# Up projection: in every second tile of weights the short matmul is issued before the long one

## The chip, the core and the metric

The kernel runs on one core of one Trainium2 chip. The metric is the device time of one execution in microseconds (us), as the median of the executions shown. The engines are TensorE (PE in the profile; its weight loads have a row of their own, PEld), VectorE (DVE), ScalarE (ACT), GpSimd (POOL) and SyncE (SP), whose queue issues the transfers of the weights.

## What is computed

One transformer block on 256 tokens of width 2048: a mixing part (three attention branches with gates) and a feed-forward part. The change lies in the feed-forward part, in the product `h2 @ w_up`:

```python
h2 = rms_norm(x, g_ffn[l])                                          # 256 x 2048
u = causal_depthwise_conv(h2 @ w_up[l], conv_w[l], conv_b[l])       # w_up: 2048 x 11264
u_gate, u_val = jnp.split(u, 2, axis=-1)
x = x + (jax.nn.silu(u_gate) * u_val) @ w_down[l]
```

All inputs are float32. The kernel splits each float32 operand of a product into a rounded part (hi) and the remainder (lo), both of type fp32r, and adds three products: hi times hi, lo times hi, hi times lo.

## The kernel before

**Tiling of the up projection (lines 729 to 745).** The product is made transposed: the weights are the stationary operand, in tiles of 128 x 128, and the tokens are the moving one. `hT` holds, for each of the 16 tiles of the contraction (`KT`), 512 columns: the hi parts of the 256 tokens and, behind them, their lo parts. The loop over `f0` takes four tiles of output columns at a time, and `s` says whether they belong to the gate half or the value half, so there are 11 x 2 = 22 groups. A group has four PSUM banks, `ps[0]` to `ps[3]`, one for each output tile `i`, and collects the 16 contraction tiles in them. There are eight banks in all, so that two groups can be in hand.

**A pair of matmuls.** For each contraction tile `k + j` and each output tile `i` two matmuls are issued (lines 739 and 740):

- the long one: stationary `hi[:, j, c]`, moving all 512 columns of `hT`; it adds hi times hi into columns 0 to 255 of the bank and hi times lo into columns 256 to 511;
- the short one: stationary `lo[:, j, c]`, moving the 256 hi columns; it adds lo times hi into columns 0 to 255 of the same bank.

Each has its own weight load. So the queue of TensorE reads long, short, long, short, through the whole stage: 22 x 16 x 4 = 1408 pairs. The first matmul into a bank (`start`) is a long one, the last (`stop`) a short one.

**Where the weights come from.** `piece` (lines 130 to 141) brings 512 KB of weights at a time, two contraction tiles by four output tiles, which feed 8 pairs. SyncE's queue issues the transfer into `raw`; ScalarE casts it into `hi` (line 136); VectorE subtracts to get `lo` (line 137). `raw`, `hi` and `lo` have four buffers each (`WBUFS`, `SBUFS`), so the cast for one piece waits until TensorE has done with the `hi` of the piece four back, and the subtraction writes the `lo` buffer of the piece four back. The stage has 22 x 8 = 176 pieces.

**What else runs in the stage.** When a group is complete, `conv` (lines 705 to 727) drains its banks: ScalarE copies columns 256 to 511 out (line 710, tile `cr`), VectorE adds columns 0 to 255 (line 712), and both engines then do the convolution, the gate and the split into `aT`. These steps are handed to `later` and issued piece by piece by `tick`. On ScalarE and VectorE they stand in the same queues as the casts and subtractions. The order on each engine is the order of the program.

**Other stages with the same kind of matmul.** `product` and `passes` (lines 143 to 166) serve the projections before: there the tokens are stationary and the weights move. Three matmuls of one width follow one another into one bank (lines 147, 148, 149), then three into the other. The width is 512 columns in nearly all of them (tiles `g`, `s`, `f`, `o`), 256 in the last product of the `s` tiles (`s4`).

Of the kernel before, what the change touches and what calls it, by code (L numbers as in the profile page):

```python
# [41 lines left out]
def hybrid_block(  # L42
# [25 lines left out]
    nc = tc.nc  # L68
# [12 lines left out]
    def bank(name):  # L81
        return pp.tile([P, 512], F32, tag="bank", name=name)
# [14 lines left out]
    def later(gen):  # L97
        waiting.append(gen)

    def tick():  # L100
        while waiting and len(active) < WINDOW:
            active.append([waiting.popleft(), 0])
        for a in list(active):
            if a[1] > 0:
                a[1] -= 1
                continue
            try:
                a[1] = next(a[0]) or 0
            except StopIteration:
                active.remove(a)  # L110
# [19 lines left out]
    def piece(src, a, n, name):  # L130
        raw = wp.tile([P, PIECE], F32, tag="raw", name=f"raw_{name}")
        hi = wp.tile([P, PIECE], F32R, tag="hi", bufs=SBUFS, name=f"hi_{name}")
        lo = wp.tile([P, PIECE], F32R, tag="lo", bufs=SBUFS, name=f"lo_{name}")
        m = a * n
        nc.sync.dma_start(raw[:, :m].rearrange("p (a n) -> p a n", a=a), src)
        pin(nc.scalar.copy(hi[:, :m], raw[:, :m]))  # L136
        pin(nc.vector.tensor_tensor(lo[:, :m], raw[:, :m], hi[:, :m].bitcast(F32), ALU.subtract))  # L137
        return (
            hi[:, :m].rearrange("p (a n) -> p a n", a=a),
            lo[:, :m].rearrange("p (a n) -> p a n", a=a),  # L140
        )
# [9 lines left out]
    def product(x_of, w, nk, n0, n, name):  # L151

        ps = [bank(f"{name}_{t}") for t in range(NT)]
        wv = w.rearrange("(k p) n -> p k n", p=P)
        for k in range(0, nk, 2):
            a = min(2, nk - k)
            wh, wl = piece(wv[:, k : k + a, n0 : n0 + n], a, n, f"{name}_{k}")
            order = [(j, t) for j in range(a) for t in range(NT)]
            if k + a == nk:
                order.sort(key=lambda jt: jt[1])  # L160
            for j, t in order:
                passes(ps[t][:, :n], x_of(k + j), t, wh[:, j], wl[:, j], k + j == 0, k + j == nk - 1)
            tick()
        return ps
# [278 lines left out]
    ps = proj(C_MQ, MEM_W, "mq")  # L443
# [33 lines left out]
    for c in range(3):  # L477
        ps = proj(c * 512, 512, f"f{c}")
# [7 lines left out]
    ps = proj(1536, 512, "f3")  # L486
# [3 lines left out]
    ps = proj(2048, 262, "f4")  # L490
# [68 lines left out]
    for c in range(3):  # L559
        ps = proj(C_SB + c * 512, 512, f"s{c}")  # L560
# [4 lines left out]
    ps = proj(C_SB + 1536, 512, "s3")  # L565
# [3 lines left out]
    ps = proj(C_SB + 2048, 256, "s4")  # L569
# [61 lines left out]
    for n in range(4):  # L631
        n0 = n * 512
        gate = []
        for b in range(3):
            bg = gp.tile([P, 512], F32, tag="bg", name=f"bg_{n}_{b}")
            nc.sync.dma_start(bg, b_gate[0, b, n0 : n0 + 512].partition_broadcast(P))
            ps = proj(C_GATE + b * D + n0, 512, f"g{n}_{b}")
# [11 lines left out]
        for i, (w, k0, nk, b) in enumerate(branches):  # L649
            ps = product(lambda k: oT[:, k0 + k], w[0], nk, n0, 512, f"b{n}_{b}")  # L650
# [10 lines left out]
    hT = xt_pool.tile([P, KT, 2 * S], F32R, tag="xt", name="hT")  # L661
# [19 lines left out]
    for n in range(4):  # L681
        c = slice(n * 512, (n + 1) * 512)
        ps = product(lambda k: mT[k // 2][:, k % 2], w_out[0], KT, n * 512, 512, f"o{n}")
# [21 lines left out]
    def conv(ps, f, s):  # L705
        if not pads:
            padded()
        ct = s * FT + f
        cr = cp.tile([P, S], F32, tag="cr", bufs=2, name=f"cr_{f}_{s}")
        nc.scalar.copy(cr, ps[:, S:])  # L710
        u = pads[f % 2]
        nc.vector.tensor_tensor(cr, cr, ps[:, :S], ALU.add)
        nc.vector.tensor_tensor(u[:, 2:], cr, rbc, ALU.mult)
        y = cp.tile([P, S], F32, tag="y", bufs=6, name=f"y_{f}_{s}")
        tap = lambda j: taps[:, j, ct : ct + 1]
        nc.scalar.activation(y, u[:, 2:], AF.Identity, scale=tap(2), bias=tap(3))
        nc.vector.scalar_tensor_tensor(y, u[:, 1 : S + 1], tap(1), y, ALU.mult, ALU.add)
        nc.vector.scalar_tensor_tensor(y, u[:, 0:S], tap(0), y, ALU.mult, ALU.add)
        if s == 0:
            nc.scalar.activation(y, y, AF.Silu)  # L720
            ys[f] = y
        else:
            g = ys.pop(f)
            nc.vector.tensor_tensor(g, g, y, ALU.mult)
            split_to(aT[:, f, :], g)
        return
        yield

    for f0 in range(0, FT, 4):
        for s in range(2):  # L730
            ps = [bank(f"u{f0 + i}_{s}") for i in range(4)]
            c0 = s * D_FF + f0 * P
            for k in range(0, KT, 2):
                hi, lo = piece(upv[:, k : k + 2, c0 : c0 + 512], 2, 512, f"u{f0}_{s}_{k}")
                for j in range(2):
                    first, last = k + j == 0, k + j == KT - 1
                    for i in range(4):
                        c = slice(i * P, (i + 1) * P)
                        nc.tensor.matmul(ps[i], lhsT=hi[:, j, c], rhs=hT[:, k + j, :], start=first, stop=False)  # L739
                        nc.tensor.matmul(  # L740
                            ps[i][:, :S], lhsT=lo[:, j, c], rhs=hT[:, k + j, :S], start=False, stop=last
                        )
                tick()
            for i in range(4):
                later(conv(ps[i], f0 + i, s))
# [180 lines left out]
```

## Time and profile before

| | us |
|---|---|
| median of three executions | 1498.22 |
| lowest and highest | 1497.55, 1498.96 |
| span of the profiled execution | 1494.4 |
| first and last start of a matmul of the up projection, in that span | 766.0, 1255.2 |
| TensorE busy in the span | 1483.2 |
| VectorE, ScalarE busy | 1014.0, 794.0 |

The profile gives for each engine the time in which at least one of its instructions was running. Matmuls are pipelined, their ends are modelled, and their times overlap, so the distance from start to start says more about them than their durations. The profiled execution's own time is its span; the device time of an execution is a little longer than the span, and the median stands 3.8 us above it.

### The profile page before, as it was taken

What the parts mean: (1) busy time and instruction counts of PE and PEld (TensorE: products, weight loads), DVE (VectorE), ACT (ScalarE), POOL (GpSimd) and SP (SyncE); (2) the same over time, 40 slices, a digit from 0 to 9 for tenths busy, and PEclk for the clock granted to TensorE, in tenths of its full rate; (3) what the DMA queues carried; (4) which work ended last, traced back from release to release, by engine and by line L of the source; (5) the groups of instructions that cost most, each with busy time, mean ns of one, the idle gap of its engine ahead of it and who ended that gap; (6) DMA issues with size and microseconds to landing.
All of it is one profiled execution on the core that took longest, in us unless ns stands there. A gap on an engine that the chain in (4) does not pass through costs nothing.

```text
span 1494.4 us, 19871 instructions
## 1 busy us (share of the span) xinstructions
PE 1483.2 (99%) x7429; PEld 1255.9 (84%) x7429; DVE 1014.0 (68%) x1465; ACT 794.0 (53%) x1108; POOL 16.1 (1%) x46
## 2 busy tenths in 40 slices
PE   8999999999999999999999999999999999999998
PEld 6888888888888888888888888888888888888777
DVE  5767566555655646555557778777778778987885
ACT  6755454358544444444456556556556656553552
POOL 0000000001000000000000000000000000000000
PEclk9999999999999999999999999999999999999999
DMA  8665475365666666655555665655656565556554
GB/s 291 193 211 158 126 220 167 119 211 164 188 194 210 185 210 203 185 190 190 184 182 183 198 191 184 196 190 184 198 187 191 186 196 183 199 188 228 185 202 140
DMA packets 138543, 283.62 MB, mean 190 GB/s; under 512 B 9275, under 2 KB 18127, under 8 KB 138447
## 3 DMA queue, kind: packets, MB, share of 16 engines
q1 hardware_dynamic: 137118, 280.26, 59.0%
q10 hardware_dynamic: 1328, 2.11, 0.4%
q8 instruction: 58, 0.95, 0.2%
q14 instruction: 39, 0.31, 0.1%
HBM read 280.23 MB, written 2.10 MB: 189 GB/s over the span
## 4 chain that ended last, share of the span: by engine, by line
PE 95%; DMA 2%; ACT 1%; DVE 1%; issue 0%; POOL 0%; SPq 0%; DVEq 0%; POOLq 0%; ACTq 0%
PE u L739 21%; PE u L740 11%; PE g L147 5%; PE g L148 5%; PE g L149 5%; PE x L797 4%; PE x L798 4%; PE x L799 4%; PE s L147 2%; PE s L149 2%; PE f L147 2%; PE f L149 2%; PE s L148 2%; PE f L148 2%; PE o L147 2%; PE o L149 2%
## 5 line engine op out<-in xcount | busy, mean ns | idle before, releaser
L739 PE MATMUL u<-hT,hi_u 128*128 128x512 f32 x1408 | 488.5, 392 | 0.0
L740 PE MATMUL u<-hT,lo_u 128*128 128x256 f32 x1408 | 395.1, 281 | 0.0
L739 PEld LDWEIGHTS u<-hT,hi_u 128*128 128x128 f32 x1408 | 263.3, 187 | 57.3
L137 DVE TENSOR_TENSOR lo_u<-raw_u,hi_u 128x1024 fp32r<-128x1024 f32 x176 | 215.4, 1224 | 116.0 <-ACT hi_u L136 115.9
L740 PEld LDWEIGHTS u<-hT,lo_u 128*128 128x128 f32 x1408 | 266.8, 189 | 0.0
L136 ACT CAST hi_u<-raw_u 128x1024 fp32r<-128x1024 f32 x176 | 184.7, 1050 | 138.4 <-PE u L739 106.5
L137 DVE TENSOR_TENSOR lo_g<-raw_g,hi_g 128x1024 fp32r<-128x1024 f32 x96 | 117.7, 1229 | 101.3 <-ACT hi_g L136 98.8
L136 ACT CAST hi_g<-raw_g 128x1024 fp32r<-128x1024 f32 x96 | 100.7, 1051 | 121.8 <-PE g L148 97.4
L147 PE MATMUL g<-hi_g,xT 128*128 128x512 f32 x384 | 151.1, 393 | 0.0
L149 PE MATMUL g<-lo_g,xT 128*128 128x512 f32 x384 | 149.8, 390 | 0.0
L148 PE MATMUL g<-hi_g,xT 128*128 128x512 f32 x384 | 149.7, 390 | 0.0
L792 ACT CAST hi_d<-raw_d 128x1024 fp32r<-128x1024 f32 (+1 forms) x88 | 86.7, 993 | 74.6 <-PE x L798 38.7
L793 DVE TENSOR_TENSOR lo_d<-raw_d,hi_d 128x1024 fp32r<-128x1024 f32 (+1 forms) x88 | 99.8, 1148 | 16.2 <-ACT hi_d L792 16.2
L797 PE MATMUL x<-hi_d,aT 128*128 128x512 f32 x268 | 104.4, 390 | 0.0
L799 PE MATMUL x<-lo_d,aT 128*128 128x512 f32 x268 | 104.4, 390 | 0.0
L798 PE MATMUL x<-hi_d,aT 128*128 128x512 f32 x268 | 104.4, 390 | 0.0
L149 PEld LDWEIGHTS g<-lo_g,xT 128*128 128x128 f32 x384 | 72.1, 188 | 15.2
L148 PEld LDWEIGHTS g<-hi_g,xT 128*128 128x128 f32 x384 | 72.2, 188 | 14.5
L147 PEld LDWEIGHTS g<-hi_g,xT 128*128 128x128 f32 x384 | 72.2, 188 | 14.6
L137 DVE TENSOR_TENSOR lo_s<-raw_s,hi_s 128x1024 fp32r<-128x1024 f32 (+1 forms) x40 | 44.7, 1118 | 37.2 <-ACT hi_s L136 37.2
L137 DVE TENSOR_TENSOR lo_f<-raw_f,hi_f 128x1024 fp32r<-128x1024 f32 (+1 forms) x40 | 44.7, 1120 | 34.5 <-ACT hi_f L136 33.0
L136 ACT CAST hi_f<-raw_f 128x1024 fp32r<-128x1024 f32 (+1 forms) x40 | 38.5, 966 | 52.5 <-PE f L148 47.6
(318 smaller groups left out, 2554.3 us busy)
## 6 DMA issues: line engine op xcount, KB each, us to landing
raw_u<-in_w_up_dram SPq DMA_DIRECT2D x176, 512.0 KB, 4.0
raw_g<-in_w_in_dram SPq DMA_DIRECT2D x96, 512.0 KB, 3.6
raw_d<-in_w_down_dram SPq DMA_DIRECT2D x88, 512.0 KB, 4.7
raw_f<-in_w_in_dram SPq DMA_DIRECT2D x32, 512.0 KB, 3.5
raw_s<-in_w_in_dram SPq DMA_DIRECT2D x32, 512.0 KB, 3.4
raw_o<-in_w_out_dram SPq DMA_DIRECT2D x32, 512.0 KB, 4.7
raw_kv<-in_w_mem_kv_dram SPq DMA_DIRECT2D x15, 512.0 KB, 5.4
raw_b<-in_w_br_fox_dram SPq DMA_DIRECT2D x12, 512.0 KB, 4.0
```

The lines of the kernel that those rows point to most:

```text
L136: pin(nc.scalar.copy(hi[:, :m], raw[:, :m]))
L137: pin(nc.vector.tensor_tensor(lo[:, :m], raw[:, :m], hi[:, :m].bitcast(F32), ALU.subtract))
L147: nc.tensor.matmul(o, lhsT=xh, rhs=wh, start=first, stop=False)
L148: nc.tensor.matmul(o, lhsT=xl, rhs=wh, start=False, stop=False)
L149: nc.tensor.matmul(o, lhsT=xh, rhs=wl, start=False, stop=last)
L739: nc.tensor.matmul(ps[i], lhsT=hi[:, j, c], rhs=hT[:, k + j, :], start=first, stop=False)
L740: nc.tensor.matmul(ps[i][:, :S], lhsT=lo[:, j, c], rhs=hT[:, k + j, :S], start=False, stop=last)
L792: nc.scalar.copy(hi[:, :n], src)
L793: nc.vector.tensor_tensor(lo[:, :n], src, hi[:, :n].bitcast(F32), ALU.subtract)
L797: nc.tensor.matmul(o, lhsT=ah, rhs=w[0], start=first, stop=False)
L798: nc.tensor.matmul(o, lhsT=al, rhs=w[0], start=False, stop=False)
L799: nc.tensor.matmul(o, lhsT=ah, rhs=w[1], start=False, stop=last)
```

## The change

In the up projection the two matmuls of a pair change places where `i` is 1 or 3, except for the first contraction tile of a group, whose long matmul must come first because it starts the bank.

```diff
                     for i in range(4):
                         c = slice(i * P, (i + 1) * P)
-                        nc.tensor.matmul(ps[i], lhsT=hi[:, j, c], rhs=hT[:, k + j, :], start=first, stop=False)
-                        nc.tensor.matmul(
+                        both = lambda last: nc.tensor.matmul(
+                            ps[i], lhsT=hi[:, j, c], rhs=hT[:, k + j, :], start=first, stop=last
+                        )
+                        half = lambda last: nc.tensor.matmul(
                             ps[i][:, :S], lhsT=lo[:, j, c], rhs=hT[:, k + j, :S], start=False, stop=last
                         )
+                        if first or i % 2 == 0:
+                            both(False)
+                            half(last)
+                        else:
+                            half(False)
+                            both(last)
```

TensorE, the second contraction tile of the first piece. `u_0_6213` to `u_0_6216` are the four banks; `hi_u` and `lo_u` are the two parts of the weights; the last figure is the moving operand, 512 columns for the long matmul and 256 for the short one. A minus is the order before, a plus the order with the change (the short matmul stands on line 740 before and on line 742 now):

```order
 L739 MATMUL u_0_6213<-hT,hi_u_0_0_6218 128x512
-L740 MATMUL u_0_6213<-hT,lo_u_0_0_6219 128x256
+L742 MATMUL u_0_6213<-hT,lo_u_0_0_6219 128x256
+L742 MATMUL u_0_6214<-hT,lo_u_0_0_6219 128x256
 L739 MATMUL u_0_6214<-hT,hi_u_0_0_6218 128x512
-L740 MATMUL u_0_6214<-hT,lo_u_0_0_6219 128x256
 L739 MATMUL u_0_6215<-hT,hi_u_0_0_6218 128x512
-L740 MATMUL u_0_6215<-hT,lo_u_0_0_6219 128x256
+L742 MATMUL u_0_6215<-hT,lo_u_0_0_6219 128x256
+L742 MATMUL u_0_6216<-hT,lo_u_0_0_6219 128x256
 L739 MATMUL u_0_6216<-hT,hi_u_0_0_6218 128x512
-L740 MATMUL u_0_6216<-hT,lo_u_0_0_6219 128x256
```

In the second and the fourth bank the short matmul moved ahead of the long one, so the queue reads long, short, short, long, and again. The last matmul of a piece is now a long one, on `hi`, where it was a short one, on `lo`.

VectorE, the subtractions of the first group's pieces, with what each waits for (the transfer, TensorE, ScalarE):

```order
 L137 TENSOR_TENSOR lo_u_0_6_6319<-raw_u_0_6_6317,hi_u_0_6_6318 128x1024 [waits DMAHW2_49,Activation_49]
-L137 TENSOR_TENSOR lo_u_0_8_6341<-raw_u_0_8_6339,hi_u_0_8_6340 128x1024 [waits DMAHW3_49,PE_49,Activation_49]
-L137 TENSOR_TENSOR lo_u_0_10_6363<-raw_u_0_10_6361,hi_u_0_10_6362 128x1024 [waits DMAHW4_49,PE_49,Activation_49]
+L137 TENSOR_TENSOR lo_u_0_8_6341<-raw_u_0_8_6339,hi_u_0_8_6340 128x1024 [waits DMAHW3_49,Activation_49]
+L137 TENSOR_TENSOR lo_u_0_10_6363<-raw_u_0_10_6361,hi_u_0_10_6362 128x1024 [waits DMAHW4_49,Activation_49]
 L174 SCALAR_TENSOR_TENSOR hT<-hT_6261,gmix_c,hT 128x256 [waits Activation_49]
```

The subtraction no longer waits for TensorE itself: the cast ahead of it waits for the last matmul of the piece four back, which covers both buffers.

ScalarE, the drain of the first group's last two banks and the cast behind it:

```order
 L716 ACTIVATE y_0_6474<-u_6459,taps 128x256 [waits DVE_49]
 L710 COPY cr_0_6501<-u_0_6215 128x256
-L710 COPY cr_0_6510<-u_0_6216 128x256 [waits PE_49]
+L710 COPY cr_0_6510<-u_0_6216 128x256
 L136 CAST hi_u_1_8_6564<-raw_u_1_8_6563 128x1024 [waits DMAHW3_49,PE_49,Activation_49]
```

The order of ScalarE's instructions, and of VectorE's, SyncE's and GpSimd's, is the same as before; only such waits differ. On TensorE no wait moved.

## Prediction

> **What bounds the kernel now.** I read the page from the top: the span, the engines, the chain that ended last, and then the groups of the two lines that the change touches.
>
> ```profile
> span 1494.4 us, 19871 instructions
> PE 1483.2 (99%) x7429; PEld 1255.9 (84%) x7429; DVE 1014.0 (68%) x1465; ACT 794.0 (53%) x1108; POOL 16.1 (1%) x46
> ...
> PE 95%; DMA 2%; ACT 1%; DVE 1%; issue 0%; POOL 0%; SPq 0%; DVEq 0%; POOLq 0%; ACTq 0%
> ...
> L739 PE MATMUL u<-hT,hi_u 128*128 128x512 f32 x1408 | 488.5, 392 | 0.0
> L740 PE MATMUL u<-hT,lo_u 128*128 128x256 f32 x1408 | 395.1, 281 | 0.0
> L739 PEld LDWEIGHTS u<-hT,hi_u 128*128 128x128 f32 x1408 | 263.3, 187 | 57.3
> ...
> L740 PEld LDWEIGHTS u<-hT,lo_u 128*128 128x128 f32 x1408 | 266.8, 189 | 0.0
> ```
>
> TensorE is busy for 99% of the span and makes up 95% of the chain of waits. Both groups of matmuls show an idle time of 0.0 ahead of them. So in this stage nothing is waited for: what counts is how soon one matmul may start after another. The durations 392 and 281 ns don't tell that, since they overlap. I take it from the timeline of the stage, by starts:
>
> ```profile
> 849.73 0.39 PE L739 MATMUL u<-hT,hi_u 128*128 128x512 f32 x1
> 849.96 0.28 PE L740 MATMUL u<-hT,lo_u 128*128 128x256 f32 x1
> 850.08 0.39 PE L739 MATMUL u<-hT,hi_u 128*128 128x512 f32 x1
> ...
> 855.97 0.39 PE L739 MATMUL u<-hT,hi_u 128*128 128x512 f32 x1
> ```
>
> From the first long matmul to the last one here there are 18 pairs in 6.24 us, 346.7 ns a pair. From long to short it is 230 ns, which leaves 116.7 ns from short to long. The view of the tile `u` gives the stage's first and last starts:
>
> ```profile
> L739 PE MATMUL u<-hT,hi_u x1408: 389/391/476, 766.0 to 1255.0; 128*128 128x512 f32 x176
> L740 PE MATMUL u<-hT,lo_u x1408: 277/281/285, 766.2 to 1255.2; 128*128 128x256 f32 x176
> ```
>
> 1408 pairs at 346.7 ns make 488.1 us, and the stage lies between the starts 766.0 and 1255.2, 489.2 us, so it is dense throughout. The view by windows says that the clock has nothing left to give (the column before the DMA share):
>
> ```profile
> 770.00:1250.00 480.00, 480.00 (x2774) 423.72 (x2773) 361.66 (x600) 284.98 (x438) 0.00 (x0) 1.00 0.60 190
> ```
>
> **The change part by part.** No matmul, no load and no transfer is added or removed. Of 1408 pairs, those with `i` 1 or 3 outside the first contraction tile of a group are turned round: 22 groups x 15 tiles x 2 = 660. Each time, a stretch of four matmuls that read long, short, long, short reads long, short, short, long, with a long one behind it. Of the four steps from start to start, one long-to-short (230) and one short-to-long (116.7) stay. The other two, again 230 and 116.7, together 346.7, become a step from short to short and a step from long to long. This stage has neither, but other stages have both.
>
> Short to short: the last product of the `s` tiles runs matmuls of 256 columns alone, the same type and the same size of stationary tile. Their count by the view of the tile `s` (32 on each of three lines, 96), then the first, the second and the last by the timeline:
>
> ```profile
> L149 PE MATMUL s<-lo_s,xT x160: 282/390/399, 196.4 to 309.6; 128*128 128x512 f32 x128, 128*128 128x256 f32 x32
> ...
> 298.21 0.28 PE L147 MATMUL s<-hi_s,xT 128*128 128x256 f32 x1
> 298.33 0.28 PE L148 MATMUL s<-hi_s,xT 128*128 128x256 f32 x1
> ...
> 309.61 0.28 PE L149 MATMUL s<-lo_s,xT 128*128 128x256 f32 x1
> ```
>
> 95 steps in 11.40 us are 120.0 ns each. Here three matmuls in a row add into one bank before the other bank's turn, so the step holds within a bank and from bank to bank.
>
> Long to long: a dense piece of the gate projections, 99 matmuls of 512 columns, first and last:
>
> ```profile
> 539.63 0.39 PE L147 MATMUL g<-hi_g,xT 128*128 128x512 f32 x1
> ...
> 561.85 0.39 PE L149 MATMUL g<-lo_g,xT 128*128 128x512 f32 x1
> ```
>
> 98 steps in 22.22 us are 226.7 ns each.
>
> So the two new steps cost 120.0 + 226.7 = 346.7 ns, and the two that they replace cost 346.7 ns. **The sum is 660 x 0.0 = 0.0 us.** This is more than a coincidence of two numbers. 256 further columns cost 226.7 - 120.0 = 106.7 ns, so 256 columns alone take 106.7 and each matmul has 13.3 ns on top, whatever its width. A pair of unlike neighbours, as it runs today, costs exactly a long one among long ones plus a short one among short ones. The 230 where 226.7 would be expected, and the 116.7 where 120.0 would be, are 3.3 ns that the short one starts later and the next long one gets back. In these rows the cost of a matmul does not depend on its neighbour.
>
> The bounds of the two unknown steps, by the nearest rows. Short to short: 120.0 by the same shape elsewhere; 116.7 if it behaves like today's short-to-long. Long to long: 226.7 by the same shape elsewhere; 230 if it behaves like today's long-to-short. The low end is 116.7 + 226.7 = 343.4, a gain of 3.3 ns or 2.2 us over 660 places. The high end is 120.0 + 230 = 350, a loss of 3.3 ns or 2.2 us. I take the middle, since those rows have both neighbours alike, as the new steps do.
>
> The second part is the release of the buffers. In a piece's last four matmuls the last long one starts one short step (120 ns) later than before and the last short one 227 ns earlier. So `hi` comes free later, `lo` earlier, and the cast that refills `hi` starts about 0.12 us later. Does that reach TensorE? ScalarE does wait there, by the view of waits in the stage and the timeline around one piece:
>
> ```profile
> ACT hi_u L136 <- PE u L739: 106.5, 93, 2.0
> ...
> 905.54 0.39 PE L739 MATMUL u<-hT,hi_u 128*128 128x512 f32 x1
> ...
> 905.89 0.39 PE L739 MATMUL u<-hT,hi_u 128*128 128x512 f32 x1
> 906.02 1.05 ACT L136 CAST hi_u<-raw_u 128x1024 fp32r<-128x1024 f32 x1 [0.58 <-PE u L739]
> ...
> 908.84 1.22 DVE L137 TENSOR_TENSOR lo_u<-raw_u,hi_u 128x1024 fp32r<-128x1024 f32 x1
> ```
>
> The long matmul at 905.54 is the last of a piece, the cast at 906.02 waited for it, and its subtraction (one other stands between them on VectorE) is done at 908.84 + 1.22 = 910.06. With four buffers the new weights are needed after three more pieces: 905.89 + 3 x 8 x 0.3467 = 914.21. That leaves 4.1 us at a place where VectorE is held up by a group's drain; a delay of 0.12 us is hidden by those three pieces. Queued behind the cast on ScalarE stand the copies that drain banks; a bank is wanted again a group later, after 64 pairs or 22.2 us. The wait for TensorE that the subtraction loses costs and brings nothing, because the cast ahead of it holds the same wait. Transfers keep their order. The end of a group is the same, too: its last bank gets its last two matmuls in the other order, and 120 ns + 392 ns (the long one's duration, behind the short one) is level with 230 + 281 ns.
>
> The sum for the profiled execution is 1494.4 + 0.0 = 1494.4 us. The median of the runs stands 3.8 us above its span, so I forecast 1498.2 us.
>
> **The rivals.**
>
> *The second of two short matmuls waits for its weights (slower).* Loads run ahead by one matmul only, by the rows of the weight loads in the up projection (first two) and in the 256-wide product (last two):
>
> ```profile
> 849.96 0.19 PEld L739 LDWEIGHTS u<-hT,hi_u 128*128 128x128 f32 x1
> 850.08 0.19 PEld L740 LDWEIGHTS u<-hT,lo_u 128*128 128x128 f32 x1
> ...
> 306.37 0.19 PEld L147 LDWEIGHTS s<-hi_s,xT 128*128 128x128 f32 x1
> 306.49 0.19 PEld L148 LDWEIGHTS s<-hi_s,xT 128*128 128x128 f32 x1
> ```
>
> A load starts when the matmul ahead of its own starts (849.96 and 850.08 are the starts of a short and a long one), so a short one has to cover the next load alone. The load is recorded with 190 ns, a short step with 120. Today each short is followed by a long's load; with the change every second one is followed by another short's. If the load had to end first, that step would be 190 instead of 120: 660 x 70 ns = 46 us, 1544 us. It decides from the point where a load takes more of the short step than the 120 ns it has. Against it: the 256-wide product has just such loads, 0.12 us apart with 0.19 us recorded, and doesn't slow down; and today's long ones start 116.7 ns after the load's start. So the record holds a tail that the next matmul need not wait for. Chance 0.05.
>
> The Trainium skill, "TensorE: Matmul & The Clock Gate", section "LDWEIGHTS (loading the stationary operand)", gives a load's time as its columns over 1.2 GHz: for 128 columns, as an estimate, 106.7 ns. By that the load fits a short step with 13 ns to spare and this rival costs nothing; by the recorded 190 ns it costs 46 us. The steps of 120.0 ns in the 256-wide product side with the skill's figure.
>
> *The later cast starves TensorE (slower).* If the 0.12 us came through to TensorE at each of 176 pieces, 176 x 0.12 = 21 us, 1519 us. It decides once the slack is used up, and the slack is 4.1 us in the piece shown, on a delay that doesn't add up from piece to piece, since each cast is timed from TensorE. Chance 0.03.
>
> *Two matmuls of one width in a row run into each other (faster).* Should the second of a like pair, which moves the same columns of `hT` as the one before, lose its 13.3 ns, two of the four steps of each stretch would be shorter: 660 x 2 x 13.3 ns = 17.6 us, 1480.6 us. For it speaks only that the 13.3 ns are unexplained, and that a change of width is seen to shift a start by 3.3 ns. Against it: the like neighbours of the `s` and `g` rows carry the full 13.3 ns. Those move other columns each time they change the contraction tile, but within a tile lines 147 and 148 move the same ones, and the step from 298.21 to 298.33 is 120 like the others. Chance 0.06.
>
> **How the numbers follow.** The forecast, no change, has 0.86; the three rivals 0.05, 0.03 and 0.06. A change below 0.2%, 3.0 us, is about what a measurement of this kernel can't tell from none; that is 4.5 ns in each of the 660 stretches, more than either bound of 3.3 ns. The range takes the bounds of 2.2 us on each side and the 0.7 us by which the runs before differ from their median: 1498.2 - 2.9 = 1495.3 to 1498.2 + 2.9 = 1501.1. It leaves the rivals out, 0.14 together. Of the forecast's 0.86, some 0.02 on the slow side lie beyond 0.2% by both bound and spread. Faster 0.06, same 0.84, slower 0.10.
>
> **What would show it.** In the profile after, the steps of the up projection by their starts: long to short 230, short to short 120, short to long 117, long to long 227, four matmuls in 693 ns, and the stage from its first to its last start again 489.2 us. The loads again start with the matmul ahead of their own. VectorE's and ScalarE's waits may shift by a tenth of a microsecond a piece without any idle time on TensorE. A short-to-short step above 124.5 ns with the others as forecast would make the prediction wrong on the slow side, and so would idle time ahead of line 739; a long-to-long step of 222 ns or less, on the fast side.

## The result and the profile after

The changed kernel takes 1500.91 us, the kernel before, run beside it, 1498.98 us (medians of 20 runs each). The ratio is 1.0015 with a 95% interval of 1.0008 to 1.0021: slower by 0.15%, or 2.2 us (1.2 to 3.1 us); the two medians lie 1.9 us apart. The change is below 0.2%, the time lies in the predicted range, but the forecast was no change, and there is one.

The page of the changed kernel, the span, the engines, the chain of waits, and the groups of the two lines (the short matmul stands on line 742 now):

```profile
span 1497.8 us, 19882 instructions
...
PE 1487.3 (99%) x7429; PEld 1254.6 (84%) x7429; DVE 1013.4 (68%) x1465; ACT 794.7 (53%) x1108; POOL 16.1 (1%) x46
...
PE 94%; DMA 2%; DVE 1%; ACT 1%; issue 1%; POOL 0%; SPq 0%; DVEq 0%; POOLq 0%
...
L739 PE MATMUL u<-hT,hi_u 128*128 128x512 f32 x1408 | 446.1, 396 | 0.0
...
L742 PE MATMUL u<-hT,lo_u 128*128 128x256 f32 x1408 | 284.3, 278 | 0.0
```

TensorE still waits for nothing ahead of either line, so the time was not lost to a late buffer. Nor was it lost to the clock, which the view by windows gives as 1.00, as before (the column before the DMA share):

```profile
770.00:1250.00 480.00, 480.00 (x2758) 418.79 (x2757) 359.44 (x599) 285.34 (x437) 0.00 (x0) 1.00 0.64 188
```

The view of the tile `u` has the stage's first and last starts:

```profile
L739 PE MATMUL u<-hT,hi_u x1408: 389/396/475, 764.1 to 1256.0; 128*128 128x512 f32 x176
L742 PE MATMUL u<-hT,lo_u x1408: 274/277/285, 764.3 to 1255.9; 128*128 128x256 f32 x176
```

The stage takes 491.9 us from 764.1 to 1256.0, where it took 489.2. That is 2.7 us, read from one profiled execution of each kernel; it lies within the interval of the change in the kernel's time. (The two profiled spans differ by 3.4 us; the other 0.7 us lie outside the stage.) The timeline shows the new order as pairs of one kind (x2). The first three rows and the last of a stretch in which no group ends:

```profile
857.07 0.62 PE L739 MATMUL u<-hT,hi_u 128*128 128x512 f32 x2
857.53 0.40 PE L742 MATMUL u<-hT,lo_u 128*128 128x256 f32 x2
857.76 0.63 PE L739 MATMUL u<-hT,hi_u 128*128 128x512 f32 x2
...
871.70 0.63 PE L739 MATMUL u<-hT,hi_u 128*128 128x512 f32 x2
```

Here are 21 stretches of four matmuls in 14.63 us, 696.7 ns each. Forecast were 2 x 346.7 = 693.3. So each of the 660 stretches costs 3.3 ns more than without the change, and 660 x 3.3 = 2.2 us of the 2.7 are found. By the starts in the trace, the four steps of these stretches average 233 ns from long to short (forecast 230), 115 from short to short (forecast 120), 116 from short to long (forecast 116.7) and 233 from long to long (forecast 226.7). The second of two short matmuls starts earlier than forecast; what is lost is lost behind the long ones.

The rest belongs to the first contraction tiles of the groups, whose order did not change, and to the turn from them to the second tile. From the second group on, a group takes 22.320 us where it took 22.187. Of these 133 ns the 30 stretches make 100; 18 lie in the first tile and some 15 at the turn behind it. The first tile of the second group, where long and short alternate, from its second long matmul to the first of the next tile:

```profile
787.87 0.40 PE L739 MATMUL u<-hT,hi_u 128*128 128x512 f32 x1
...
788.93 0.40 PE L739 MATMUL u<-hT,hi_u 128*128 128x512 f32 x1
```

These three pairs stand in the same order as before the change. They take 1.06 us, 353 ns each; in the kernel before, a pair of the second group takes 347. An unchanged order runs slower. No price put on each changed place can explain that, and it is the first hint of the cause.

**A second look at the trace before.** The same slower pairs stand there, too, in the stage's first microseconds (first and last row ahead of the eight transposes, the transposes, and first and last row of a stretch behind them):

```profile
766.02 0.39 PE L739 MATMUL u<-hT,hi_u 128*128 128x512 f32 x1
...
771.31 0.40 PE L739 MATMUL u<-hT,hi_u 128*128 128x512 f32 x1
...
771.66 1.04 PE L184 MATMUL hT<-ident,xres 128*128 128x128 f32 x8
772.45 0.48 PE L739 MATMUL u<-hT,hi_u 128*128 128x512 f32 x1
...
773.58 0.39 PE L739 MATMUL u<-hT,hi_u 128*128 128x512 f32 x1
...
783.29 0.39 PE L739 MATMUL u<-hT,hi_u 128*128 128x512 f32 x1
```

From 766.02 to 771.31 there are 15 pairs in 5.29 us, 352.7 ns a pair; from 773.58 to 783.29 there are 28 pairs in 9.71 us, 346.8. They are the same lines in the same order, once at 353 and once at 347 ns. The kernel before spends nearly the whole stage in the faster of two rhythms.

Slow steps stand in that trace also where all matmuls have one width. In the gate projections, the first and the last start of a stretch shortly behind four transposes:

```profile
425.94 0.39 PE L148 MATMUL g<-hi_g,xT 128*128 128x512 f32 x1
...
428.26 0.39 PE L149 MATMUL g<-lo_g,xT 128*128 128x512 f32 x1
```

These ten steps take 2.32 us, 232 ns each, though nothing is waited for between them. Behind them the run settles at 226.7 ns and stays there for hundreds of matmuls; the prediction took its row from the middle of such a settled run. Whether these first steps and the slow rhythm have one cause is not shown.

### The profile page after: what moved, and what is told of

The parts are those of the page before. It is cut to its first block, busy times and chain, and to the rows that moved or that the text cites. A ratio compares the mean times of both kernels' runs of the same rounds, so it can differ in the third digit from the quotient of the medians.

```text
span 1497.8 us, 19882 instructions
## 1 busy us (share of the span) xinstructions
PE 1487.3 (99%) x7429; PEld 1254.6 (84%) x7429; DVE 1013.4 (68%) x1465; ACT 794.7 (53%) x1108; POOL 16.1 (1%) x46
## 4 chain that ended last, share of the span: by engine, by line
PE 94%; DMA 2%; DVE 1%; ACT 1%; issue 1%; POOL 0%; SPq 0%; DVEq 0%; POOLq 0%
PE u L739 22%; PE u L742 11%; PE g L147 5%; PE g L148 5%; PE g L149 5%; PE x L805 4%; PE x L806 4%; PE x L807 4%; PE s L147 2%; PE s L149 2%; PE f L147 2%; PE f L148 2%; PE s L148 2%; PE f L149 2%; PE o L147 2%; PE o L149 2%
## 5 line engine op out<-in xcount | busy, mean ns | idle before, releaser
L739 PE MATMUL u<-hT,hi_u 128*128 128x512 f32 x1408 | 446.1, 396 | 0.0
L742 PE MATMUL u<-hT,lo_u 128*128 128x256 f32 x1408 | 284.3, 278 | 0.0
L136 ACT CAST hi_u<-raw_u 128x1024 fp32r<-128x1024 f32 x176 | 184.7, 1049 | 144.5 <-PE u L739 119.9
L739 PEld LDWEIGHTS u<-hT,hi_u 128*128 128x128 f32 x1408 | 217.9, 189 | 4.1
```

The source lines that it names most:

```text
L739: both = lambda last: nc.tensor.matmul(ps[i], lhsT=hi[:, j, c], rhs=hT[:, k + j, :], start=first, stop=last)
L742: half = lambda last: nc.tensor.matmul(ps[i][:, :S], lhsT=lo[:, j, c], rhs=hT[:, k + j, :S], start=False, stop=last)
```

## The experiments

Four theories were set against each other. Theories 1 to 3 charge each place: 1, the second of two short ones waits for its weight load; 2, two long ones side by side cost more; 3, a long matmul right after a short one into the same bank costs more. Theory 4, formed after the first four runs: the alternating stream has two stable rhythms, 346.7 and 353.3 ns a pair, and what breaks the alternation can throw it from one into the other. In the diffs, `both(i)` issues the long matmul and `half(i)` the short one; those of e1 and e6 stand against the changed kernel, the others against the kernel before, and e4 has the changed order. Each experiment is one execution, so it is read by the starts inside its trace.

**Short first everywhere (e1).**

```diff
-                        if first or i % 2 == 0:
+                        if first:
                             both(False)
                             half(last)
                         else:
                             half(False)
                             both(last)
```

> Every pair but those of a group's first contraction tile has the short matmul first, so no two of a kind stand side by side, but in 15 of 16 tiles all four banks get a long matmul right after a short one. Theory 1 (two short ones side by side: the second waits for its weight load): no excess, a piece of 16 matmuls takes 2773 ns as before and the stage 489.2 us. Theory 2 (two long ones side by side cost more): the same, 489.2 us. Theory 3 (a long matmul right after a short one into the same bank costs about 3.3 ns more, wherever it stands): twice as many such places as in the changed kernel, about 5 us of excess, stage 494.6 us.

The view of `u`:

```profile
L738 PE MATMUL u<-hT,hi_u x1408: 389/398/403, 764.9 to 1263.0; 128*128 128x512 f32 x176
L743 PE MATMUL u<-hT,lo_u x1408: 274/281/366, 765.1 to 1262.9; 128*128 128x256 f32 x176
```

The stage takes 498.1 us, 8.9 more than before, and the one run of the kernel 1507.6 us against 1499.96. Theories 1 and 2 fall in their simple form: there are like neighbours only where a group begins and behind its first tile. Theory 3 forecast 494.6, and alone would stand closest, but the run below with no such places contradicts it. What this run shows is a stream that alternates and still costs 6 ns a pair too much (8.9 us over 1408 pairs), the same as the first pairs of the kernel before. It is not slow throughout, though. In the first group, behind two transposes, from one long matmul to another:

```profile
783.42 0.40 PE L738 MATMUL u<-hT,hi_u 128*128 128x512 f32 x1
...
787.58 0.40 PE L738 MATMUL u<-hT,hi_u 128*128 128x512 f32 x1
```

Here 12 pairs take 4.16 us, 346.7 ns each, in the same order, short ahead of long in one bank. The next group is slow again. So this order, too, has both rhythms, and no charge for the order within a bank can explain that.

**Long, long, short, short (e2), and four and four (e3).**

```diff
-                    for i in range(4):
-                        both(i)
-                        half(i, last)
+                    for i in (0, 2):
+                        both(i)
+                        both(i + 1)
+                        half(i, last)
+                        half(i + 1, last)
```

```diff
-                    for i in range(4):
-                        both(i)
-                        half(i, last)
+                    for i in range(4):
+                        both(i)
+                    for i in range(4):
+                        half(i, last)
```

> Long, long, short, short over two banks at a time: as many like neighbours as in the changed kernel, but no bank gets a long matmul right after a short one, and every bank gets its long one first. Theories 1 and 2 (like neighbours): the excess of the changed kernel, a piece of 2787 ns instead of 2773, stage 491.9 us or a little more. Theory 3 (order within the bank): none, 489.2 us.

> Four long matmuls, then four short ones for each contraction tile: per eight matmuls three steps from short to short and three from long to long, where the changed kernel has two of each. Theories 1 and 2, if each step of like neighbours costs the same: 1.5 times the excess, 10 ns per eight matmuls, a piece of 2793 ns, stage 493.2 us. Theory 1 with waits that pile up over a run of short ones: more than that. Theory 3: none, 489.2 us. If rows of other stages hold (like neighbours at 227 and 120 ns in long runs, free of any excess): one excess at the turn from one kind to the other alone, less than in the changed kernel.

The view of `u`, of the first and of the second:

```profile
L738 PE MATMUL u<-hT,hi_u x1408: 389/396/477, 764.4 to 1255.5; 128*128 128x512 f32 x176
L743 PE MATMUL u<-hT,lo_u x1408: 274/277/284, 764.8 to 1255.8; 128*128 128x256 f32 x176
```

```profile
L738 PE MATMUL u<-hT,hi_u x1408: 386/396/486, 764.6 to 1258.9; 128*128 128x512 f32 x176
L743 PE MATMUL u<-hT,lo_u x1408: 277/281/286, 765.5 to 1259.5; 128*128 128x256 f32 x176
```

Pairs of banks: 764.4 to 1255.8, 491.4 us, 2.2 over before. No long matmul follows a short one into its bank here, so theory 3 is out as the cause; an excess of 2.2 us would fit theories 1 and 2. Four and four: 764.6 to 1259.5, 494.9 us, 5.7 over before. Theories 1 and 2 at an equal charge forecast 493.2. The excess does not follow the count of like neighbours: 1.5 times as many give 2.6 times as much, and almost none (e1) give four times as much.

**288 columns in the short matmul, in the changed order (e4) and in the order before (e11).**

```diff
-                            ps[i][:, :S], lhsT=lo[:, j, c], rhs=hT[:, k + j, :S], start=False, stop=last
+                            ps[i][:, : S + 32], lhsT=lo[:, j, c], rhs=hT[:, k + j, : S + 32], start=False, stop=last
```

> The order of the changed kernel with 288 instead of 256 columns in the short matmul (32 columns more of lo times lo are computed than the reference needs). Theory 1: a short step is now 133 ns, and a weight load of some 113 ns from start to start fits with 20 ns to spare, so the excess is gone: per eight matmuls 4 x 226.7 + 4 x 133.3 = 1440.0 ns, a piece of 2880 ns. Theories 2 and 3: the excess of 6.7 ns per eight stays, a piece of 2893 ns.

> The order of the kernel before, with 288 columns in the short matmul (as in the earlier run on the changed order). Without excess a pair takes 226.7 + 133.3 = 360.0 ns and a group 23.04 us. If alternation alone is what spares the excess: 23.04 us. If the kernel before is in a rhythm that happens to fit 512 and 256 columns: some excess, as in the changed order with 288 (23.31 us).

The view of `u`, changed order, then order before:

```profile
L738 PE MATMUL u<-hT,hi_u x1408: 387/395/476, 765.2 to 1278.7; 128*128 128x512 f32 x176
...
L743 PE MATMUL u<-hT,lo_u x1408: 290/295/299, 765.4 to 1278.6; 128*128 128x288 f32 x176
```

```profile
L738 PE MATMUL u<-hT,hi_u x1408: 389/395/477, 765.1 to 1277.4; 128*128 128x512 f32 x176
L743 PE MATMUL u<-hT,lo_u x1408: 292/295/297, 765.3 to 1277.6; 128*128 128x288 f32 x176
```

32 further columns should add 1408 x 13.3 ns = 18.8 us to 489.2, 508.0 us. The changed order takes 513.5 us, an excess of 5.5 us that is larger than with 256 columns, although each short step now gives a load 13 ns more. Theory 1 is refuted: the step from short to short averages 133 ns here by the starts in the trace, with no excess over 133.3, and in the changed kernel it was 115. The order before takes 512.5 us, an excess of 4.5 us: alternation alone does not spare it. That the kernel before has next to none goes with its widths of 512 and 256, and with the faster of two rhythms.

**One swap, one pause (e5).**

```diff
             ps = [bank(f"u{f0 + i}_{s}") for i in range(4)]
+            if (f0, s) == (24, 0):
+                for _ in range(2):
+                    nc.tensor.transpose(ps[0][:, :P], xres[:, 0, :P], ident)
...
-                        both(i)
-                        half(i, last)
+                        if (f0, s, k, j, i) == (4, 0, 2, 0, 1):
+                            half(i)
+                            both(i, last)
+                        else:
+                            both(i)
+                            half(i, last)
```

> The kernel before, with one single pair turned round (in the third group, f0 = 4, s = 0) and two transposes of 128 columns put ahead of the first matmul of the thirteenth group (f0 = 24, s = 0); what they write is overwritten at once by that group's first matmul. Theory 4 (the alternating stream has two stable rhythms, 346.7 and 353.3 ns a pair; two like neighbours throw it into the slow one, and a pause such as transposes lets it fall into the fast one): a group takes 22.187 us before the swap, then 22.61 us in each group from the swap to the transposes, and 22.187 us again behind them; the stage is some 4 us longer than 489.2. Theories 1 to 3 in any form that charges each place by itself: a few ns for the one swap, some 0.3 us for the transposes, every other group 22.187 us, stage 489.5 us.

The timeline around the one swap (the rows with x2); the rows left out are pairs in alternation:

```profile
804.66 0.39 PE L741 MATMUL u<-hT,hi_u 128*128 128x512 f32 x1
...
813.67 0.39 PE L741 MATMUL u<-hT,hi_u 128*128 128x512 f32 x1
813.90 0.40 PE L746 MATMUL u<-hT,lo_u 128*128 128x256 f32 x2
814.14 0.62 PE L741 MATMUL u<-hT,hi_u 128*128 128x512 f32 x2
...
814.71 0.40 PE L741 MATMUL u<-hT,hi_u 128*128 128x512 f32 x1
...
827.78 0.40 PE L741 MATMUL u<-hT,hi_u 128*128 128x512 f32 x1
```

Ahead of the swap 26 pairs take 9.01 us, 346.5 ns each; behind it 37 pairs take 13.07 us, 353.2 ns each, through the end of the group and on into the next. The stage as a whole takes 497.9 us (by the view of `u`, 765.3 to 1263.2), 8.7 over before; the two transposes account for some 0.2 of it. Theories 1 to 3 allowed 489.5. One swapped pair among 1408 costs more than 660 of them. That settles that the excess of the alternating stream is a state of the stream and no charge by place. By the starts in the trace, the step from short to long averages 116.7 ns on both sides of the swap; the step from long to short is 230 ns ahead of it and then goes through 241, 236 and 233 in turn. Nearly all weight loads start within 5 ns of the matmul ahead of their own, in both rhythms. The pause of two transposes, which theory 4 expected to bring the fast rhythm back, did not.

**The changed order with pauses (e6).**

```diff
+            if (f0, s) != (0, 0):
+                for _ in range(2):
+                    nc.tensor.transpose(ps[0][:, :P], xres[:, 0, :P], ident)
```

> The order of the changed kernel, with two transposes ahead of every group but the first (overwritten at once). Theory 4: a group's first contraction tile, which alternates, runs at 1386.7 ns after its first steps instead of 1404, the 27 ns at the turn to the second tile shrink, and the other tiles keep 1393.3 ns, since their like neighbours come again and again. Charge by place: the same 1404 ns in the first tile.

The timeline from one such pause (line 735) to the group's second tile, the short matmuls left out:

```profile
855.48 0.38 PE L735 MATMUL u<-ident,xres 128*128 128x128 f32 x2
...
856.04 0.39 PE L741 MATMUL u<-hT,hi_u 128*128 128x512 f32 x1
...
857.10 0.40 PE L741 MATMUL u<-hT,hi_u 128*128 128x512 f32 x1
```

From 856.04 to 857.10 there are three pairs at 353 ns. The first tile stayed slow: theory 4 as put there, with a pause as the cure, missed again. (The stage takes 496.5 us; 21 pauses of some 0.22 us each explain what it has over the changed kernel.)

**Two long and one short (e7), two short and one long (e8).**

```diff
-                    for i in range(4):
-                        both(i)
-                        half(i, last)
+                    for i in (0, 2):
+                        both(i, last)
+                        both(i + 1)
+                        half(i + 1, last)
```

```diff
-                    for i in range(4):
-                        both(i)
-                        half(i, last)
+                    for i in (0, 2):
+                        if first:
+                            both(i)
+                            both(i + 1)
+                        half(i, last)
+                        half(i + 1)
+                        if not first:
+                            both(i + 1, last)
```

> Long, long, short: the short matmul (lo times hi) is left out for every second output tile, so there are steps from long to long but none from short to short. Three matmuls at 226.7 + 226.7 + 120.0 would be 573.3 ns without any excess. Theory 1 (short to short alone costs): 573.3. Theory 2 (long to long costs): over 576. Theory 4: the rhythm may have an excess of its own, since widths are mixed, but no load is late anywhere.

> Short, short, long: the long matmul is left out for every second output tile (but in a group's first contraction tile), so there are steps from short to short but none from long to long. Three matmuls at 120.0 + 120.0 + 226.7 would be 466.7 ns without any excess. Theory 1: 470 ns or more. Theory 2: 466.7. Theory 4: some excess is possible, as in the other mixed rhythms.

The timeline of the first (34 triples from first to last row), then of the second (4 triples to the middle row, 10 more to the last; a wait of TensorE ends just ahead of it):

```profile
899.92 0.63 PE L738 MATMUL u<-hT,hi_u 128*128 128x512 f32 x2
900.38 0.28 PE L743 MATMUL u<-hT,lo_u 128*128 128x256 f32 x1
...
919.86 0.39 PE L738 MATMUL u<-hT,hi_u 128*128 128x512 f32 x1
```

```profile
1134.83 0.39 PE L738 MATMUL u<-hT,hi_u 128*128 128x512 f32 x1
...
1136.73 0.39 PE L738 MATMUL u<-hT,hi_u 128*128 128x512 f32 x1
...
1141.40 0.39 PE L738 MATMUL u<-hT,hi_u 128*128 128x512 f32 x1
```

19.94 us / 34 = 586.5 ns where 573.3 would be free of excess: 13 ns for each triple, twice the slow rhythm's charge for a pair, and no two short ones ever meet. The second takes 1.90 us / 4 = 475 ns behind the wait and then 4.67 us / 10 = 467.0, where 466.7 would be free of it: its first triples are slow, but it settles without any excess, as the stream of one width did. (In its stage as a whole TensorE waits for weights, so the stage's length tells nothing.) So a mixture need not have an excess. Taken alone these two runs fit theory 2, but the slow alternation of e1 and e5 keeps its excess through hundreds of pairs without two long ones side by side.

**Several swaps and pauses (e9).**

```diff
+            for _ in range({1: 2, 3: 8, 6: 4, 9: 1, 12: 3, 15: 6, 18: 5}.get(f0 // 2 + s, 0)):
+                nc.tensor.transpose(ps[0][:, :P], xres[:, 0, :P], ident)
...
+                        if (f0 // 2 + s) in (2, 5, 8, 11, 14, 17) and (k, j, i) == (2, 0, 1):
+                            half(i)
+                            both(i, last)
+                        else:
+                            both(i)
+                            half(i, last)
```

> The kernel before with one swapped pair in each of six groups (the 3rd, 6th, 9th, 12th, 15th and 18th) and, ahead of each group that follows one of them, a run of f32 transposes: 8, 4, 1, 3, 6 and 5 of them; two more transposes stand ahead of the 2nd group, before any swap. Theory 4a (any pause restores the fast rhythm): all groups behind a pause at 22.19 us. Theory 4b (a pause restores it only when the stream comes out of it at a certain moment, as the first such pause of the kernel before did and the one of the last series didn't): some lengths restore it and some don't. Theory 4c (the fast rhythm is not restored by transposes at all, something else in the first piece did it): none does, 22.61 us in every group from the first swap on.

The timeline around the swap in the twelfth group:

```profile
1007.76 0.40 PE L740 MATMUL u<-hT,hi_u 128*128 128x512 f32 x1
...
1016.95 0.40 PE L740 MATMUL u<-hT,hi_u 128*128 128x512 f32 x1
1017.18 0.40 PE L745 MATMUL u<-hT,lo_u 128*128 128x256 f32 x2
1017.42 0.64 PE L740 MATMUL u<-hT,hi_u 128*128 128x512 f32 x2
...
1018.36 0.39 PE L740 MATMUL u<-hT,hi_u 128*128 128x512 f32 x1
...
1027.72 0.39 PE L740 MATMUL u<-hT,hi_u 128*128 128x512 f32 x1
```

Ahead of the swap 26 pairs take 9.19 us, 353.5 ns each; behind it 27 pairs take 9.36 us, 346.7. Here the swap brought the fast rhythm, where in e5 it brought the slow one. The same happened in the groups of the next two swaps, while the second swap turned fast into slow, and the first and the third changed nothing. The pauses were no better: two and eight transposes left a fast stream fast, three, six and five turned a fast one slow, four and one left a slow one slow. So 4a is refuted, and so is 4c's forecast of slow groups from the first swap on, since stretches behind a swap ran fast. Theory 4b is nearest, though in this run no pause brought the fast rhythm back; it was behind pauses that the fast rhythm began in the first groups of the kernel before and of e1. It goes for swaps as for pauses: a break in the alternation may turn the rhythm either way or leave it.

**Banks apart (e10), other columns (e12).**

```diff
                     for i in range(4):
                         both(i)
-                        half(i, last)
+                        if owed:
+                            half(*owed.pop())
+                        owed.append((lo[:, j, i * P : (i + 1) * P], k + j, i, last))
+                    if last:
+                        half(*owed.pop())
```

```diff
-                            ps[i][:, :S], lhsT=lo[:, j, c], rhs=hT[:, k + j, :S], start=False, stop=last
+                            ps[i][:, :S], lhsT=lo[:, j, c], rhs=hT[:, k + j, S:], start=False, stop=last
```

> Long and short alternate as before, but the short matmul of a bank is issued after the next bank's long one, so that two matmuls in a row never write one bank, but at a group's end. At each group's start two long ones stand side by side. If the slow rhythm comes from two matmuls in a row on one bank: no slow rhythm, 22.19 us a group and 489.2 us in all or less. If the banks have nothing to do with it (theory 4): the like neighbours at each group's start bring the slow rhythm, 22.61 us a group, 498 us.

> The kernel before with the one swapped pair in the third group and no further pause; in every short matmul the moving operand is columns 256 to 511 of the token tile instead of 0 to 255 (so lo times lo stands in the place of lo times hi). If the slow rhythm comes from reading the same columns in neighbouring matmuls: no slow rhythm behind the swap, 22.19 us a group. Theory 4, widths alone: 22.19 us in the first two groups, 22.61 us from the swap to the end, the stage about 8.7 us longer than 489.2.

The view of `u`, banks apart, then other columns (which has e5's one swap, but no pause):

```profile
L739 PE MATMUL u<-hT,hi_u x1408: 389/398/477, 765.3 to 1263.4; 128*128 128x512 f32 x176
L744 PE MATMUL u<-hT,lo_u x1408: 277/281/284, 765.7 to 1263.7; 128*128 128x256 f32 x176
```

```profile
L738 PE MATMUL u<-hT,hi_u x1408: 389/398/476, 765.1 to 1262.6; 128*128 128x512 f32 x176
L743 PE MATMUL u<-hT,lo_u x1408: 277/281/284, 765.4 to 1262.8; 128*128 128x256 f32 x176
```

Banks apart takes 498.4 us and other columns 497.7 us, 9.2 and 8.5 over before. The slow rhythm is there without neighbours on one bank, and without neighbours that read the same columns. Neither is needed for it.

Other columns also shows that a turn of the rhythm is not chance. It and e5 ran on two chips and read different columns in the short matmuls, yet all starts of their first eleven groups, the swap and the slow rhythm included, agree within 1 ns when counted from the stage's first. In the first two groups both agree as closely with the kernel before.

## Why the prediction was wrong

**What bounds the kernel: right.** TensorE waits for nothing in the stage, before or after. The order of the queue and the 660 places are as counted.

**The release of the buffers: right.** The cast waits a little longer for TensorE (119.9 us in the stage against 106.5), and none of it reaches TensorE, whose idle time ahead of lines 739 and 742 is 0.0.

**The cost of the two new steps: wrong.** The step that failed is "In these rows the cost of a matmul does not depend on its neighbour", and with it the sum of 660 x 0.0 us. Measured were 3.3 ns for each stretch of four, 2.2 us, and some 0.5 us more in the first tiles and the turns behind them. The step from short to short came out at 115 ns instead of 120.0, the one from long to long at 233 instead of 226.7, and the step from long to short, which was to stay at 230, at 233. The rows of 120.0 and 226.7 ns were right for settled streams of one width, and the pair of 346.7 was right for most of the stage, but their agreement holds for the fast rhythm of the alternating stream alone. I read it as a law of single matmuls. The counter-evidence lay in the same trace: the stage took 489.2 us where 1408 pairs at 346.7 make 488.1, and I passed over the 1.1 us as dense. The transposes in the first group explain most of it; the first pairs at 352.7 ns explain 0.1 us of it, and would have shown that the same instructions can run at two speeds. So would the first ten steps of a run of the gate projections, at 232 ns.

**The size.** The upper bound, 2.2 us from "today's long-to-short" of 230 ns, met the 2.2 us of the stretches by accident. It stood for 230 ns from long to long with 120 from short to short. Measured were 233 and 115, both outside the bounds that the prediction gave these steps, and e5 shows for the alternating stream that no fixed cost by place holds. The prediction also took a change below 0.2% for about what can't be told from none; 20 runs of each kernel told 0.15%.

**The rivals.** The late load of the second short matmul did not come: that matmul started 115 ns after the first, earlier than forecast. In e4, with 13 ns more for each load, the excess grew, and in e7 there is an excess without any two short ones side by side. The load of 106.7 ns that the prediction took as an estimate from the Trainium skill, "TensorE: Matmul & The Clock Gate", section "LDWEIGHTS (loading the stationary operand)", is not contradicted: the shortest step behind a short matmul in the changed kernel is 112 ns. The starving of TensorE did not happen, and the like neighbours gained nothing in sum: the 5 ns that the short ones came earlier were lost on the long ones.

**What stays open.** Which part of TensorE has the two rhythms is not known. A late load behind a short matmul, two matmuls in a row on one bank, the order within a bank and re-read columns are not needed for an excess; what is left is anything that depends on the widths in turn. What the other engines read and write at the time was not varied by itself; that e5 and e12 agree within 1 ns speaks against a part in it that changes from run to run. Nor is it known what decides which way a break turns the rhythm, and why the order long, short, short, long settles at a rate of its own. What is shown is that one break of the alternation can be enough to lose the fast rhythm (e5), and that long, long, short, short, which breaks it as often in another order, costs nearly the same as the change (e2, 491.4 us against 491.9). That the 348.3 ns a pair of the changed order is what such breaks settle at when they come in every stretch is an inference from these two, and e8, which has like neighbours in every triple and settles without excess, shows that it doesn't hold for every mixture.

## What to carry to other kernels

When matmuls of two widths alternate in a dense stream, its rate may be one of several, and one row of the trace, or a sum of costs by instruction, doesn't tell which: compare the starts over the whole stage, its first microseconds too. A change of order that costs nothing by such a sum can take the stream out of a rhythm that nothing in the program secured; here a single swapped pair cost 8.5 us (e12) and 660 of them 2.7 us. In this trace a stream of 512 columns alone was slow for some ten steps behind a break and then settled, so a row from the middle of such a stream does not vouch for a mixture.

## What the runs showed of the hardware that was not expected

An alternating stream of 512 and 256 columns runs at 346.7 or at 353.3 ns a pair, for hundreds of pairs without change, in one and the same program, with nothing waited for (e5, e9). Three of six single swaps turned it from slow to fast (e9), and the outcome repeats within 1 ns on another chip (e5, e12). Mixtures in other orders have rates of their own: 348.3 ns a pair in the changed kernel (696.7 / 2), and 586.5 ns for two long and one short, 13 more than the widths alone would take. Two short and one long settle at 467.0, no more than the widths alone take (e8). Matmuls of 512 columns alone start some ten steps at 232 ns behind transposes and settle at 226.7 (the kernel before).
